# Norm chains of w_out moved under the following products, and first products of six weight pairs kept in DRAM, in a fused decoder layer

## Chip, cores and metric

The kernel runs on one core of a Trainium2 chip. The metric is the device time of one execution in microseconds.

## What is computed

One layer of a hybrid decoder for 1024 prompt tokens and 32 sample tokens (8 sequences of 4), 1056 columns in all, in float32. Two attention branches are merged to `m`, and then, cut to what the change touches:

```python
y = m @ w_out                                  # 1024 x 1024
x = x + gt_m * rmsnorm(y, g_post_mix)          # first norm
h2 = rmsnorm(x, g_pre_mlp) * (1 + sc_f) + sh_f # second norm
u = square(relu(h2 @ w_up))                    # 1024 x 4096
x = x + gt_f * rmsnorm(u @ w_down, g_post_mlp)
```

## The kernel before, in words

Everything here is kept with features on the 128 partitions and tokens along the columns. The 1056 tokens are two halves of TH = 528, each worked in two sub-chunks of TQ = 264 columns. A float32 product is three matmuls on operands split into a high and a low part (high by high, high by low, low by high). `raw_w` (L1224) loads weights on SP's queue into `raw`, of which there are three slots, and `split4` (L1229) makes the parts `ph` (a cast on ACT, L1233) and `pl` (a subtraction, L1235, two in three on POOL, the third on DVE), six slots each.

The stage has these parts, written in this order.

- For each half: the **w_out GEMM**. For each of 8 feature blocks and each sub-chunk, 24 matmuls (L1335 to L1337) go into one PSUM bank `ps_g`, of which there are three; such 24 are called a group. ACT copies a bank to Q (L1323) and squares it (L1325, L1328), POOL adds the squares to `ssq` (L1329).
- Then x of that half is loaded and turned by 40 transposes on PE into banks `ps_t` (L1348), copied on ACT (L1349).
- Then the **norm chain** of that half. `rstd` (L1255) sums `ssq` over partitions with PE products into `ps_o` (L1261), forms rv on DVE (L1262) and the power rt on POOL (L1263). `rstd_bc` broadcasts it with PE products into `ps_s` (L1275) and copies it to `r` on ACT (L1276). Then for 8 blocks: the scaling on DVE (`scaled`, L1286, and L1288 and L1282 for the sample columns), the add of x (L1355, in turn on DVE and POOL), the square on ACT (L1360) and its add to a second `ssq` (L1361, in turn POOL and DVE), and a store of x1 (L1363). Then the second sum and broadcast, 8 scalings, 8 shifts on ACT (L1368). `part` (L1305) splits an operand of 4 blocks by 528 columns into high (ACT, L1307) and low (DVE, L1308); the first half's two operands are split at the chain's end.
- The **up stage** works on 16 pairs of feature blocks of w_up by a Strassen-like scheme with 7 products per pair. A product (`product`, L1403) is 24 matmuls, 12 into each of two banks (L1410 to L1412). The first two products of a pair need only the first half's operands (0 and 1 in `hi`, `lo`), so `first_two` (L1419) forms them for the first PRE = 4 pairs ahead of the rest; it keeps the first in `s` in SBUF and reads the second with `s` added on DVE (L1431). `operands` (L1379) then builds the others (T1 to T4, B22) from both halves: one subtraction on POOL (L1383, t3), three on DVE (L1384 to L1386), each 2112 columns, then five `part`s. `pair` (L1436) does the other products: four sums S of the weights on DVE (L1439 to L1442), the products, reads (L1452 to L1458, L1483), relu and square on ACT (L1415, L1416) and a store to `d_u`. The weight pairs' banks come from all eight PSUM banks in turn (`bank8`).

Each engine takes its instructions in one order, set by a scheduler that goes by the written order, priorities and its own estimate of times; SP's queue holds all loads and stores here. A tile waits until its slot's last user is done, so a group of the GEMM waits until its bank was copied.

Of the kernel before, what the change touches and what calls it, by code (L numbers as in the profile page):

```python
# [18 lines left out]
P = 128  # L19
# [8 lines left out]
CQ = tuple((a, a + TQ) for a in range(0, T, TQ))  # L28
PRE = 4
NPC = 6  # L30
# [35 lines left out]
def hybrid_kernel(ctx: ExitStack, tc: tile.TileContext, ins, outs):  # L66
# [1224 lines left out]
    def mg_h(k, a, b):  # L1291
        return MG[a // TQ][0][:, k]
# [3 lines left out]

    TH = T // 2
    Q = []
# [10 lines left out]

    for th in range(2):  # L1310
        a, b = th * TH, (th + 1) * TH
        m = min(b, NP) - a
        Q.append([xs(qp, F32) for _ in range(2)])
        Y = lambda ft: Q[th][ft // 4][:, ft % 4]
        ssq = sums(npl, TH)
        for fp in range(4):
            wr = raw_w(w_out, 0, 8, fp * 2 * P, 2 * P)
            for ft in (2 * fp, 2 * fp + 1):
                pieces = [split4(wr[:, 4 * kh:4 * kh + 4, (ft % 2) * P:(ft % 2 + 1) * P]) for kh in range(2)]

                def evac(a_, b_, o):
                    c = slice(a_ - a, b_ - a)
                    act.copy(Y(ft)[:, c], o)  # L1323
                    if ft == 0:
                        act.activation(ssq[:, c], o, AF.Square)  # L1325
                    else:
                        sq = tl(npl, [P, TQ], F32, "sq", 2)
                        act.activation(sq, o, AF.Square)  # L1328
                        pool.tensor_tensor(ssq[:, c], ssq[:, c], sq, ALU.add)  # L1329

                for a_, b_ in CQ[2 * th:2 * th + 2]:
                    o = bank("g")[:, :TQ]
                    for k in range(8):
                        (wh, wl), kk = pieces[k // 4], k % 4
                        pe.matmul(o, wh[:, kk], mg_h(k, a_, b_), start=(k == 0), stop=False)  # L1335
                        pe.matmul(o, wh[:, kk], mg_l(k, a_, b_), start=False, stop=False)
                        pe.matmul(o, wl[:, kk], mg_h(k, a_, b_), start=False, stop=(k == 7))  # L1337
                    evac(a_, b_, o)
        xT = [xs(mgp if th else qp, F32) for _ in range(2)]
        for t0, t1 in tok_tiles(a, b):  # L1340
            w_ = t1 - t0
            for q in range(2):
# [6 lines left out]
                act.copy(xT[q][:, :, t0 - a:t1 - a], pt[:, :, :w_])  # L1349
        r = rstd_bc(npl, ssq, TH)  # L1350
        ssq2 = sums(npl, TH)
        for ft in range(8):
            y = Y(ft)
            scaled(y, r, gt_m, ft, m, TH)
            (pool if ft % 2 else dve).tensor_tensor(y, y, xT[ft // 4][:, ft % 4], ALU.add)  # L1355
            if ft == 0:
                act.activation(ssq2[:, :TH], y, AF.Square)
            else:
                sq = tl(npl, [P, TH], F32, "sq2", 2)
                act.activation(sq, y, AF.Square)  # L1360
                (dve if ft % 2 else pool).tensor_tensor(ssq2[:, :TH], ssq2[:, :TH], sq, ALU.add)  # L1361
            if ft % 4 == 3:
                sp.dma_start(d_x1[:, ft - 3:ft + 1, a:b], Q[th][ft // 4])  # L1363
        r2 = rstd_bc(npl, ssq2, TH)
        for ft in range(8):
            y = Y(ft)
# [7 lines left out]
    nps.close()  # L1374

    _mark(nc, "up")

# [14 lines left out]

    stg = ExitStack()
    sgp = stg.enter_context(tc.tile_pool(name="sgp", bufs=1, reuse_waits="tile"))
    bank_n = [0]

    def bank8():

        bank_n[0] += 1
        return bank("gggsstto"[bank_n[0] % 8])  # L1400

    SUB = ((0, TQ), (TQ, TH))

    def product(accs_, w, x, first):

        wh, wl = w
        for (s0, s1), acc in zip(SUB, accs_):
            o = acc[:, :TQ]
            for k in range(4):
                pe.matmul(o, wh[:, k], hi[x][:, k, s0:s1], start=first and k == 0, stop=False, skip_group_check=True)  # L1410
                pe.matmul(o, wh[:, k], lo[x][:, k, s0:s1], start=False, stop=False, skip_group_check=True)  # L1411
                pe.matmul(o, wl[:, k], hi[x][:, k, s0:s1], start=False, stop=k == 3, skip_group_check=True)  # L1412

# [4 lines left out]

    def first_two(i):  # L1419

        wr = raw_w(w_up, 0, 8, 2 * i * P, P)
        A11, A12 = split4(wr[:, 0:4]), split4(wr[:, 4:8])
        ab, bb = [bank8() for _ in SUB], [bank8() for _ in SUB]
        s = tl(sgp, [P, TH], F32, "s", PRE)
        c11 = tl(sgp, [P, TH], F32, "c", 3)
        product(ab, A11, 0, True)
        for (s0, s1), acc in zip(SUB, ab):
            act.copy(s[:, s0:s1], acc[:, :TQ])  # L1428
        product(bb, A12, 1, True)
# [3 lines left out]
        return s  # L1433

    def pair(i, s=None):
        wr = raw_w(w_up, 0, 8, 2 * i * P, 2 * P)  # L1436
# [22 lines left out]

        quad = lambda: tl(sgp, [P, TH], F32, "c", 3)  # L1460
        pre = s is not None
        if not pre:
# [28 lines left out]

    kept = [first_two(i) for i in range(PRE)]
    operands()
    for i in range(FF // (2 * P)):
        pair(i, kept[i] if i < PRE else None)
    stg.close()
    qps.close()
# [107 lines left out]
    def finish_cm(a, b, ssq):  # L1605
# [3 lines left out]
        x1 = load_x1(a, b)  # L1609
        r = rstd_bc(xw, ssq, n)  # L1610
        for ft in range(8):
# [54 lines left out]
```

## Time and profile before

| | us |
|---|---|
| median of 3 runs | 1942.78 |
| lowest, highest | 1940.33, 1943.16 |
| profiled execution | 1948.05 |
| its span | 1946.3 |
| PE busy | 1831.2 (94%) |
| DVE, ACT, POOL busy | 907.5 (47%), 860.6 (44%), 491.5 (25%) |

The span goes from the first profiled instruction to the last; the execution's own time holds 1.75 us more around it. A busy time is the union of an engine's instructions. An instruction's row gives its start counted from the span's start. The time of a matmul in a row holds its latency, so matmuls overlap: their pace is read from their starts or from a count in a window.

### The profile page before, as it was taken

Reading aid. Unit: us, or ns where it says so; the run is one execution under the profiler, and the core shown is the slowest. Engines: PE = TensorE matmul, PEld = TensorE weight load, DVE = VectorE, ACT = ScalarE, POOL = GpSimd, SP = SyncE. Lnnn points to the kernel's source line nnn. Section 1 sums busy time; section 2 is a strip of 40 time slices with the busy share of each in tenths; the row PEclk is TensorE's granted clock in tenths of the full one; section 3 lists DMA queues with packets and bytes.
Section 4 is the critical chain, followed back from the end, with each engine's and each line's share of the span. In section 5 each row is a group of like instructions: output and inputs, shape, how many; then the busy total and the mean of one; then the engine's idle time right before and its main releaser. Section 6 shows DMA issues by size and latency. Waiting matters only on the chain. (4 is left out here: it accounts for less than half of the span.)

```text
span 1946.3 us, 30982 instructions
## 1 busy us (share of the span) xinstructions
PE 1831.2 (94%) x12353; PEld 1723.1 (89%) x12353; DVE 907.5 (47%) x1907; ACT 860.6 (44%) x1553; POOL 491.5 (25%) x436
## 2 busy tenths in 40 slices
PE   6899999999999999999999494899999899999998
PEld 3888789998888999899999494899999799999997
DVE  3654545554455655544561416843333314344436
ACT  4556545657555434433124444555555531112212
POOL 3200010001233211101165344323222432222213
PEclk9899989999999999998999796999999899999999
DMA  8321422123547211353234322333233422222113
GB/s 268 77 68 59 149 77 77 54 75 111 175 165 217 78 49 57 106 177 120 58 101 162 132 77 87 102 100 121 95 100 121 172 88 89 88 101 98 67 42 138
DMA packets 178793, 209.09 MB, mean 107 GB/s; under 512 B 13908, under 2 KB 140432, under 8 KB 178648
## 3 DMA queue, kind: packets, MB, share of 16 engines
q1 hardware_dynamic: 173560, 190.13, 30.5%
q0 software_dynamic: 4864, 16.91, 2.6%
q8 instruction: 97, 1.59, 0.3%
q14 instruction: 48, 0.39, 0.1%
q10 hardware_dynamic: 224, 0.06, 0.0%
HBM read 163.40 MB, written 43.67 MB: 106 GB/s over the span
## 5 line engine op out<-in xcount | busy, mean ns | idle before, releaser
L404 PE MATMUL ps_g<-Xh,wh 128*128 128x352 f32 (+1 forms) x1176 | 393.7, 335 | 1.5 <-ACT wh L265 1.4
L406 PE MATMUL ps_g<-Xh,wl 128*128 128x352 f32 (+1 forms) x1176 | 390.4, 333 | 0.0
L405 PE MATMUL ps_g<-Xl,wh 128*128 128x352 f32 (+1 forms) x1080 | 356.7, 330 | 0.4 <-DVE Xl L347 0.4
L404 PEld LDWEIGHTS ps_g<-Xh,wh 128*128 128x128 f32 (+1 forms) x1176 | 222.7, 189 | 8.0 <-issue 3.0
L406 PEld LDWEIGHTS ps_g<-Xh,wl 128*128 128x128 f32 (+1 forms) x1176 | 221.8, 189 | 6.2 <-issue 4.2
L404 PE MATMUL ps_g<-uh,ph 128*128 128x352 f32 x672 | 218.0, 326 | 8.4 <-ACT uh L1518 7.7
L405 PE MATMUL ps_g<-ul,ph 128*128 128x352 f32 x672 | 216.8, 323 | 1.3 <-POOL ul L1519 1.3
L406 PE MATMUL ps_g<-uh,pl 128*128 128x352 f32 x672 | 216.5, 322 | 0.0
L405 PEld LDWEIGHTS ps_g<-Xl,wh 128*128 128x128 f32 (+1 forms) x1080 | 204.0, 189 | 5.9 <-issue 3.9
L1235 POOL TENSOR_TENSOR pl<-raw,ph 128x512 fp32r<-128x512 f32 x92 | 126.9, 1381 | 299.7 <-ACT ph L1233 299.7
L1233 ACT CAST ph<-raw 128x512 fp32r<-128x512 f32 x136 | 84.0, 621 | 253.1 <-PE ps_g L405 171.0
L266 POOL TENSOR_TENSOR wl<-wr,wh 128x1024 fp32r<-128x1024 f32 x26 | 63.1, 2425 | 441.8 <-ACT wh L265 295.2
L1534 DVE TENSOR_TENSOR acc<-acc,ps_g 128x352 f32<-128x352 f32 x144 | 74.0, 519 | 162.7 <-PE ps_g L406 150.6
L404 PEld LDWEIGHTS ps_g<-uh,ph 128*128 128x128 f32 x672 | 127.1, 190 | 9.6 <-ACT uh L1518 7.9
L405 PEld LDWEIGHTS ps_g<-ul,ph 128*128 128x128 f32 x672 | 127.2, 189 | 1.7 <-POOL ul L1519 1.7
L406 PEld LDWEIGHTS ps_g<-uh,pl 128*128 128x128 f32 x672 | 126.9, 189 | 0.0
L1410 PE MATMUL ps_g<-X,ph 128*128 128x264 f32 x340 | 98.4, 290 | 6.9 <-ACT s L1428 4.1
L1411 PE MATMUL ps_g<-X,ph 128*128 128x264 f32 x340 | 98.8, 291 | 2.3 <-DVE X L1308 2.3
L1412 PE MATMUL ps_g<-X,pl 128*128 128x264 f32 x340 | 98.3, 290 | 0.0
L1235 DVE TENSOR_TENSOR pl<-raw,ph 128x512 fp32r<-128x512 f32 x44 | 34.9, 793 | 126.5 <-ACT ph L1233 120.4
L1335 PE MATMUL ps_g<-X,ph 128*128 128x264 f32 x256 | 75.2, 294 | 17.0 <-ACT ssq L1325 10.8
L1235 POOL TENSOR_TENSOR pl<-S,ph 128x512 fp32r<-128x512 f32 x42 | 54.9, 1309 | 135.0 <-ACT ph L1233 135.0
(619 smaller groups left out, 4524.8 us busy)
## 6 DMA issues: line engine op xcount, KB each, us to landing
wr<-in_w_in SPq DMA_DIRECT2D x44, 512.0 KB
d_u<-c SPq DMA_DIRECT2D x64, 264.0 KB
ul<-d_u SPq DMA_DIRECT2D x32, 528.0 KB
wr<-in_w_ada SPq DMA_DIRECT2D x32, 512.0 KB
raw<-in_w_up SPq DMA_DIRECT2D x16, 1024.0 KB
raw<-in_w_down SPq DMA_DIRECT2D x16, 1024.0 KB
d_sg<-sgo SPq DMA_DIRECT2D x60, 176.0 KB
raw<-in_w_out SPq DMA_DIRECT2D x8, 1024.0 KB
```

Of the source, the lines that this page charges most:

```text
L266: (dve if lo_turn[0] % 2 else pool).tensor_sub(wl, wr, f(wh))
L404: pe.matmul(o, wh[:, k], rh(k, a, b), start=(k == 0), stop=False)
L405: pe.matmul(o, wh[:, k], rl(k, a, b), start=False, stop=False)
L406: last = pe.matmul(o, wl[:, k], rh(k, a, b), start=False, stop=(k == nk - 1))
L1233: act.copy(h_, src)
L1235: (dve if turn[0] % 3 == 0 else pool).tensor_sub(l_, src, f(h_))
L1335: pe.matmul(o, wh[:, kk], mg_h(k, a_, b_), start=(k == 0), stop=False)
L1410: pe.matmul(o, wh[:, k], hi[x][:, k, s0:s1], start=first and k == 0, stop=False, skip_group_check=True)
L1411: pe.matmul(o, wh[:, k], lo[x][:, k, s0:s1], start=False, stop=False, skip_group_check=True)
L1412: pe.matmul(o, wl[:, k], hi[x][:, k, s0:s1], start=False, stop=k == 3, skip_group_check=True)
L1534: dve.tensor_tensor(accs[a // 352](ft), accs[a // 352](ft), o, ALU.add)
```

## The change

- The norm chain of each half becomes a generator in steps (`norms`), and so do the transposes (`turn_x`). The steps of the first half's chain are written within the second half's GEMM, after the groups named in NORM_AT; those of the second half's within the first products, after the products named in NORM2_AT; the transposes after the second group of the blocks in XT_AT. `issue_after` holds a step's instructions behind the matmul given.
- The GEMM's banks are copied on DVE instead of ACT, and the squares read the copy.
- PRE goes from 4 to 6. `s` is stored to DRAM (`d_s`) and loaded again by `pair`. The first products use banks `g` and `t` alone.
- `raw` has two slots for three. One tag `n` of 8 slots of 528 columns and one tag `v` of 4 serve r, squares, s and c in both stages.
- `part` of the first half is called inside its chain, each operand as soon as its four blocks are done.

```diff
-PRE = 4
+PRE = 6
+NORM_AT = ((0, 0), (0, 1), (2, 1), (3, 1), (4, 0), (4, 1))
+XT_AT = (3, 4, 5, 6, 7)
+NORM2_AT = (0, 1, 4, 5, 6, 7)
...
-        wr = tl(w2p, [P, nk, n], F32, "raw", 3)
+        wr = tl(w2p, [P, nk, n], F32, "raw", 2)
...
+    def after(ins):
+        return tc.issue_after(ins) if ins is not None else nullcontext()
...
+    def norms(th):
+        rt = rstd(ssqs[th], TH)
+        yield
+        r = rstd_bc(npl, rt, TH)
+        ssq2 = sums(npl, TH)
         for ft in range(8):
-            y = Y(ft)
+            y = Y(th, ft)
             scaled(y, r, gt_m, ft, m, TH)
...
-                sq = tl(npl, [P, TH], F32, "sq2", 2)
+                sq = tl(npl, [P, TH], F32, "n", 8)
...
-        r2 = rstd_bc(npl, ssq2, TH)
+        yield
+        rt = rstd(ssq2, TH)
+        yield
+        r2 = rstd_bc(npl, rt, TH)
         for ft in range(8):
...
-        if th == 0:
-            for kq in range(2):
-                part(kq, Q[0][kq], qp, mgp)
+            if th == 0 and ft % 4 == 3:
+                part(ft // 4, Q[0][ft // 4], qp, mgp)
+        yield
...
-                    act.copy(Y(ft)[:, c], o)
+                    dve.tensor_copy(y, o)
...
-                        act.activation(sq, o, AF.Square)
+                        act.activation(sq, y, AF.Square)
...
+                    with after(last.ins):
+                        if (ft, si) in NORM_AT:
+                            next(chain, None)
+                        if si and ft in XT_AT:
...
+                            next(turns[th], None)
+        for _ in chain:
+            pass
+        for _ in turns[th]:
+            pass
+        chain = norms(th)
...
-    def first_two(i):
+    def first_two(i, n_):
...
-        ab, bb = [bank8() for _ in SUB], [bank8() for _ in SUB]
+        ab, bb = [bank8("gggtt") for _ in SUB], [bank8("gggtt") for _ in SUB]
...
+        last = product(ab, A11, 0, True)
+        step(last, 2 * n_)
...
+        last = product(bb, A12, 1, True)
+        step(last, 2 * n_ + 1)
...
+        sp.dma_start(d_s[n_], s)
...
+        if pre:
+            s = tl(npl, [P, TH], F32, "n", 8)
+            sp.dma_start(s, d_s[i])
...
+    def step(last, at):
+        if at in NORM2_AT:
+            with after(last):
+                next(chain, None)
...
-    kept = [first_two(i) for i in range(PRE)]
+    for i in range(PRE):
+        first_two(i, i)
+    for _ in chain:
+        pass
     operands()
```

The order of the instructions up to the middle of the first GEMM, and from the start of the down stage on, is the same in both. Between them it shows the move best at three places. In the rows that follow a tile carries its number, and the lines are those of the file they come from.

The first place is PE in the second GEMM, at the first chain's second sum (`ps_o`) and broadcast (`ps_s`). Before, they follow the transposes after the GEMM's third group:

```order
L1348 MATMUL ps_t_11637<-u_4_82,S_11635 128x128 x4
L1261 MATMUL ps_o_11045<-u_7_91,ssq_11003 128x1 x5
L1275 MATMUL ps_s_11056<-u_4_82,rt_11047 128x128 x4
L1275 MATMUL ps_s_11062<-u_4_82,rt_11047 128x16
L1335 MATMUL ps_g_11194<-X_9712,ph_11157 128x264
```

Now they stand at the end of the eleventh group (`ps_g_11468`), with one matmul between them:

```order
L1386 MATMUL ps_g_11468<-X_9710,ph_11464 128x264
L1387 MATMUL ps_g_11468<-X_9711,ph_11464 128x264
L1266 MATMUL ps_o_11248<-u_7_91,ssq_11072 128x1 x5
L1388 MATMUL ps_g_11468<-X_9710,pl_11465 128x264
L1279 MATMUL ps_s_11325<-u_4_82,rt_11250 128x128 x4
L1279 MATMUL ps_s_11331<-u_4_82,rt_11250 128x16
L1386 MATMUL ps_g_11497<-X_9712,ph_11460 128x264
```

So the sum moved behind eight more groups, and the broadcast has one matmul to cover rv and rt.

The second place is the queue that evacuates the GEMM's banks just after that broadcast. Before it is ACT, where the first copies of the second GEMM stand behind the shifts and the two casts:

```order
L1276 COPY r_11055<-ps_s_11062 128x16
L1368 ACTIVATE X_10365<-X_10365,mod_24_175 128x528 x4
L1368 ACTIVATE X_10366<-X_10366,mod_24_175 128x528
L1307 CAST X_11081<-X_10365 128x2112
L1368 ACTIVATE X_10366<-X_10366,mod_24_175 128x528 x3
L1307 CAST X_11085<-X_10366 128x2112
L1323 COPY X_11089<-ps_g_11103 128x264
```

Now it is DVE, where the copies of the ninth to eleventh group stand behind the eight scalings and the first low part:

```order
L1267 TENSOR_SCALAR rv_11249<-ps_o_11248 128x5
L1290 SCALAR_TENSOR_TENSOR X_10366<-X_10366,mod_25_176,n_11324 128x528 x4
L1290 SCALAR_TENSOR_TENSOR X_10367<-X_10367,mod_25_176,n_11324 128x528 x4
L1312 TENSOR_TENSOR X_11343<-X_10366,X_11342 128x2112
L1391 COPY X_10985<-ps_g_11386 128x264
L1391 COPY X_10985<-ps_g_11415 128x264
L1391 COPY X_10985<-ps_g_11468 128x264
L1312 TENSOR_TENSOR X_11355<-X_10367,X_11354 128x2112
```

So three copies passed from behind the whole chain on ACT to the middle of its last step on DVE.

The third place is DVE in the first products, at the first sum of squares of the second chain. Before, its adds are alone between the adds of x and rv:

```order
L1355 TENSOR_TENSOR X_11090<-X_11090,X_11626 128x528 x2
L1361 TENSOR_TENSOR ssq_11729<-ssq_11729,sq_2145_11740 128x528
L1361 TENSOR_TENSOR ssq_11729<-ssq_11729,sq_2147_11754 128x528
L1361 TENSOR_TENSOR ssq_11729<-ssq_11729,sq_2149_11769 128x528
L1361 TENSOR_TENSOR ssq_11729<-ssq_11729,sq_2151_11783 128x528
L1262 TENSOR_SCALAR rv_11788<-ps_o_11787 128x5
L1439 TENSOR_TENSOR S_12342<-raw_12340 128x512
```

Now the reads of the first pairs' second banks (`ps_t_11722` and on), a split and the S add of pair 0 stand among them:

```order
L1349 TENSOR_TENSOR X_10985<-X_10985,X_11359 128x528 x2
L1355 TENSOR_TENSOR ssq_11796<-ssq_11796,n_11807 128x528
L1467 TENSOR_TENSOR n_11725<-ps_t_11722,n_11724 128x264
L1467 TENSOR_TENSOR n_11725<-ps_t_11723,n_11724 128x264
L1355 TENSOR_TENSOR ssq_11796<-ssq_11796,n_11821 128x528
L1467 TENSOR_TENSOR n_11875<-ps_g_11872,n_11874 128x264
L1355 TENSOR_TENSOR ssq_11796<-ssq_11796,n_11836 128x528
L1467 TENSOR_TENSOR n_11875<-ps_t_11873,n_11874 128x264
L1239 TENSOR_TENSOR pl_12143<-raw_12136,ph_12142 128x512
L1355 TENSOR_TENSOR ssq_11796<-ssq_11796,n_11850 128x528
L1475 TENSOR_TENSOR S_12307<-raw_12305 128x512
L1267 TENSOR_SCALAR rv_11973<-ps_o_11972 128x5
```

So rv stands behind an add that needs pair 0's weights, and the banks of the second product are read after the chain's scalings and adds. On PE the fourth product's second bank (`ps_t_11873`) is the one of `ps_t_11722`.

## Rows read from the trace of the kernel before

**Rows 1.** The page's strip: the busy tenths of PE in forty equal slices of the span, 48.7 us each.

```profile
PE   6899999999999999999999494899999899999998
```

**Rows 2.** Windows, each with the busy time and the instructions of the engines, then PE's granted clock as a share of full speed, the share of the DMA engines and GB/s.

```profile
1087.84:1121.52 33.68, 6.78 (x37) 5.82 (x37) 20.58 (x23) 16.03 (x25) 11.99 (x9) 0.57 0.31 112
1121.52:1162.00 40.48, 40.48 (x315) 40.48 (x316) 4.54 (x5) 17.75 (x44) 21.31 (x22) 0.93 0.23 64
1175.22:1232.80 57.58, 26.58 (x160) 25.13 (x159) 40.70 (x79) 27.05 (x43) 25.86 (x14) 0.70 0.25 89
1260.00:1500.00 240.00, 240.00 (x1972) 240.00 (x1971) 84.43 (x159) 134.39 (x261) 70.71 (x55) 1.00 0.33 108
1500.00:1538.00 38.00, 37.87 (x311) 37.65 (x310) 8.13 (x17) 20.59 (x43) 11.62 (x10) 1.00 0.36 121
```

**Rows 3.** The waits of PE from 1024 to 1260 us: who waited for whom, us in total, times, the longest.

```profile
PE ps_o L1261 <- DVE ssq L1361: 33.2, 2, 19.8
PE ps_g L1335 <- ACT ssq L1325: 10.8, 1, 10.8
```

**Rows 4.** PE's timeline at the two chains: start, us from the first one's start to the last one's end, line, operation, tiles, count; in brackets the idle time before and what ended it. L1335 to L1337 are the w_out GEMM, L1348 the transposes of x, L1261 and L1275 the column sum and the broadcast, L1410 to L1412 the products of w_up.

```profile
1072.87 1.04 PE L1348 MATMUL ps_t<-u,S 128*128 128x128 f32 x8
1073.66 0.37 PE L1335 MATMUL ps_g<-X,ph 128*128 128x264 f32 x1
1073.87 0.50 PE L1261 MATMUL ps_o<-u,ssq 128*128 128x1 f32 x4
...
1108.07 2.61 PE L1275 MATMUL ps_s<-u,rt 128*128 128x128 f32 x10 [1.52 <-POOL rt L1263]
...
1121.91 0.42 PE L1336 MATMUL ps_g<-X,ph 128*128 128x264 f32 x1
1122.13 0.42 PE L1337 MATMUL ps_g<-X,pl 128*128 128x264 f32 x1
...
1169.88 1.38 PE L1275 MATMUL ps_s<-u,rt 128*128 128x128 f32 x10
...
1232.80 0.59 PE L1411 MATMUL ps_g<-X,ph 128*128 128x264 f32 x1 [2.32 <-DVE X L1308]
```

**Rows 5.** DVE's timeline in the first chain: L1286 the scalings, L1355 the adds of x, L1308 the low half of an operand.

```profile
1084.76 7.60 DVE L1286 SCALAR_TENSOR_TENSOR X<-X,mod,r 128x528 f32<-128x528 f32 x8
1092.28 4.76 DVE L1355 TENSOR_TENSOR X<-X,X 128x528 f32<-128x528 f32 x4
...
1110.93 5.52 DVE L1286 SCALAR_TENSOR_TENSOR X<-X,mod,r 128x528 f32<-128x528 f32 x8 [4.18 <-ACT r L1276]
1117.05 2.36 DVE L1308 TENSOR_TENSOR X<-X,X 128x2112 fp32r<-128x2112 f32 x1 [0.60 <-ACT X L1307]
```

**Rows 6.** ACT's timeline: the split of the second w_out load, then the copies of r and the first evacuation after the chain.

```profile
1027.14 1.14 ACT L1233 CAST ph<-raw 128x512 fp32r<-128x512 f32 x2 [0.78 <-DMA raw<-in_w_out]
...
1110.19 0.71 ACT L1276 COPY r<-ps_s 128x512 f32<-128x512 f32 x2 [7.49 <-PE ps_s L1275]
...
1120.80 0.37 ACT L1323 COPY X<-ps_g 128x264 f32<-128x264 f32 x1
```

**Rows 7.** POOL's timeline: a split, a partial sum of squares, four adds of x, and a split in the second chain.

```profile
1038.90 1.29 POOL L1235 TENSOR_TENSOR pl<-raw,ph 128x512 fp32r<-128x512 f32 x1 [2.03 <-ACT ph L1233]
1040.15 0.75 POOL L1329 TENSOR_TENSOR ssq<-ssq,sq 128x264 f32<-128x264 f32 x1
...
1088.51 6.72 POOL L1355 TENSOR_TENSOR X<-X,X 128x528 f32<-128x528 f32 x4 [6.34 <-ACT X L1349]
...
1175.84 1.26 POOL L1235 TENSOR_TENSOR pl<-raw,ph 128x512 fp32r<-128x512 f32 x1 [6.91 <-ACT ph L1233]
```

**Rows 8.** DVE's timeline in the second chain: L1286 and L1288 the scalings, L1361 the adds of the squares, L1431 the read of two banks into c, L1384 the first difference of the operands, L1439 to L1442 the S of a pair, L1308 the low half of T2.

```profile
1172.97 0.73 DVE L1286 SCALAR_TENSOR_TENSOR X<-X,mod,r 128x496 f32<-128x496 f32 x1
...
1175.86 1.28 DVE L1288 TENSOR_TENSOR X<-X,r 128x32 f32<-128x32 f32 x1
...
1186.78 0.69 DVE L1361 TENSOR_TENSOR ssq<-ssq,sq 128x528 f32<-128x528 f32 x1
...
1194.28 0.71 DVE L1361 TENSOR_TENSOR ssq<-ssq,sq 128x528 f32<-128x528 f32 x1 [1.47 <-POOL ssq L1361]
...
1203.02 0.73 DVE L1286 SCALAR_TENSOR_TENSOR X<-X,mod,r 128x496 f32<-128x496 f32 x1
...
1211.43 0.42 DVE L1431 TENSOR_TENSOR c<-ps_s,s 128x264 f32<-128x264 f32 x1
...
1217.51 3.43 DVE L1384 TENSOR_TENSOR X<-X,X 128x2112 f32<-128x2112 f32 x1 [4.23 <-POOL X L1383]
...
1221.21 1.44 DVE L1441 TENSOR_TENSOR S<-raw 128x512 f32<-128x512 f32 x1
...
1228.39 1.75 DVE L1442 TENSOR_TENSOR S<-raw,S 128x512 f32<-128x512 f32 x1
...
1230.40 2.34 DVE L1308 TENSOR_TENSOR X<-X,X 128x2112 fp32r<-128x2112 f32 x1
```

**Rows 9.** SP's queue: the first loads of w_out, and one period of the steady pairs.

```profile
1018.57 2.15 SPq L1226 DMA_DIRECT2D raw<-in_w_out  x3
...
1459.50 0.38 SPq L1226 DMA_DIRECT2D raw<-in_w_up  x1
1460.06 17.91 SPq L1417 DMA_DIRECT2D d_u<-c  x4
```

More of the change, by code (lines that the diff above doesn't have):

```diff
@@ L1308, in part, with turn_x @@
         dve.tensor_sub(lo[name], x, f(hi[name]))
-    for th in range(2):
-        a, b = th * TH, (th + 1) * TH
[L1312 to L1322, printed above, removed]
-                    act.copy(Y(ft)[:, c], o)
[L1324 to L1327, printed above, removed]
-                        act.activation(sq, o, AF.Square)
[L1329 to L1339, printed above, removed]
+    def after(ins):
+        return tc.issue_after(ins) if ins is not None else nullcontext()
+    Y = lambda th, ft: Q[th][ft // 4][:, ft % 4]
+    ssqs = {}
+    def turn_x(th):
+        a, b = th * TH, (th + 1) * TH
+        xT = xTs[th]
         for t0, t1 in tok_tiles(a, b):
@@ L1370, in hybrid_kernel @@
                 per_seq(y, y, sh_f, ft, m, TH, ALU.add)
-        if th == 0:
-            for kq in range(2):
-                part(kq, Q[0][kq], qp, mgp)
-    nps.close()
+            if th == 0 and ft % 4 == 3:
+                part(ft // 4, Q[0][ft // 4], qp, mgp)
+        yield
+    xTs, turns = {}, {}
+    chain = iter(())
+    for th in range(2):
+        a = th * TH
+        Q.append([xs(qp, F32) for _ in range(2)])
+        ssq = ssqs[th] = sums(npl, TH)
+        for fp in range(4):
+            wr = raw_w(w_out, 0, 8, fp * 2 * P, 2 * P)
+            for ft in (2 * fp, 2 * fp + 1):
+                pieces = [split4(wr[:, 4 * kh:4 * kh + 4, (ft % 2) * P:(ft % 2 + 1) * P]) for kh in range(2)]
+                for si, (a_, b_) in enumerate(CQ[2 * th:2 * th + 2]):
+                    o = bank("g")[:, :TQ]
+                    for k in range(8):
+                        (wh, wl), kk = pieces[k // 4], k % 4
+                        pe.matmul(o, wh[:, kk], mg_h(k, a_, b_), start=(k == 0), stop=False)
+                        pe.matmul(o, wh[:, kk], mg_l(k, a_, b_), start=False, stop=False)
+                        last = pe.matmul(o, wl[:, kk], mg_h(k, a_, b_), start=False, stop=(k == 7))
+                    c = slice(a_ - a, b_ - a)
+                    y = Y(th, ft)[:, c]
+                    dve.tensor_copy(y, o)
+                    if ft == 0:
+                        act.activation(ssq[:, c], y, AF.Square)
+                    else:
+                        sq = tl(npl, [P, TQ], F32, "v", 4)
+                        act.activation(sq, y, AF.Square)
+                        pool.tensor_tensor(ssq[:, c], ssq[:, c], sq, ALU.add)
+                    with after(last.ins):
+                        if (ft, si) in NORM_AT:
+                            next(chain, None)
+                        if si and ft in XT_AT:
+                            if th not in turns:
+                                xTs[th] = [xs(mgp if th else qp, F32) for _ in range(2)]
+                                turns[th] = turn_x(th)
+                            next(turns[th], None)
[4 more added lines that the diff above has]
+        chain = norms(th)
     _mark(nc, "up")
@@ L1391, in operands, with bank8 @@
         part("B22", B22, qp, qp)
-    stg = ExitStack()
-    sgp = stg.enter_context(tc.tile_pool(name="sgp", bufs=1, reuse_waits="tile"))
     bank_n = [0]
-    def bank8():
+    def bank8(which="gggsstto"):
         bank_n[0] += 1
-        return bank("gggsstto"[bank_n[0] % 8])
+        return bank(which[bank_n[0] % len(which)])
     SUB = ((0, TQ), (TQ, TH))
@@ L1432, in first_two, with pair @@
         u_out(c11, 2 * i, 0)
-        return s
-    def pair(i, s=None):
+        sp.dma_start(d_s[n_], s)
+    def pair(i, pre):
         wr = raw_w(w_up, 0, 8, 2 * i * P, 2 * P)
@@ L1458, in add @@
                 dve.tensor_tensor(c[:, s0:s1], acc[:, :TQ], tiles[what, n_], ALU.add)
-        quad = lambda: tl(sgp, [P, TH], F32, "c", 3)
-        pre = s is not None
+        quad = lambda: tl(npl, [P, TH], F32, "n", 8)
         if not pre:
@@ L1609, in finish_cm @@
         x1 = load_x1(a, b)
-        r = rstd_bc(xw, ssq, n)
+        r = rstd_bc(xw, rstd(ssq, n), n)
         for ft in range(8):
```

29 lines of the change are left out of this document (15 added, 14 removed).

## The prediction

> **What bounds the kernel now.** I read the page's strip of forty slices first: PE is the bound, busy for nine tenths or more of nearly every slice, and outside the ramps at both ends its two worst slices, the 23rd and the 25th with a 4, lie in the stage that the change touches [rows 1]. Cutting that stage into windows says what is lost there [rows 2]. From 1260 to 1500 us, in the steady pairs, PE is never idle: 1972 matmuls of 264 columns in 240 us, 0.122 us each, so a group of 24 into one PSUM bank is 2.92 us. From 1087.84 to 1121.52 PE works 6.78 us of 33.68, and from 1175.22 to 1232.80 26.58 of 57.58. The two losses are the two norm chains, one for each half of the tokens. The waits name what PE sat for: 33.2 us for the sum of squares, 10.8 for an ACT evacuation that stood behind the chain [rows 3].
>
> PE's timeline fixes two anchors [rows 4]. The first w_out GEMM ends by about 1073.0. At 1232.80 PE starts the first matmul that had waited for the low half of T2. Between them lie 159.8 us: 89.0 to 1162, where the second GEMM ends, and 70.8 after it. In the same rows matmuls follow each other by 0.22 us after a long wait, against 0.12 otherwise; the granted clock was 0.57 in the first idle window and 0.70 in the second [rows 2], that is, partly at the lower level of 1.2 GHz.
>
> **The change, first piece (first chain, under the second GEMM).** PE's work is the same; only where it stands moves.
> - The first GEMM now carries its 40 transposes. Eight take 0.79 us, from 1072.87 to 1073.66 [rows 4], so 40 take 4.0.
> - The second GEMM is 16 groups, 46.7 us, with another 40 transposes, 4.0, and two rounds of column sum and broadcast. At full clock 4 of the 10 sum products take 0.50 with their latency, so some 0.9 for 10 in a stream, and the 10 of the broadcast 1.3 [rows 4]: a round is 2.2 and two 4.4. Together 55.1.
> - The first scaling of the chain stands on DVE ahead of the evacuation of the second GEMM's fourth group, with the first add: 8 scalings of 0.95 and an add of 1.19, as they ran beside POOL adds [rows 5], and the new PSUM copy. For that copy the bounds are 0.37, ACT's copy of the same tile [rows 6], and 0.42, DVE's read of the same bank shape [rows 8]; I take 0.42, the same engine. From the broadcast's end DVE needs 0.8 + 7.6 + 1.2 + 0.4 = 10.0, and PE has 19 matmuls and two groups in the other banks, 8.1. Wait: 1.9.
> - The sum of squares alternates DVE and POOL, 2.18 us for each pair of adds (0.71 on DVE after a wait of 1.47 for POOL, [rows 8]). r comes 12.5 us into the second GEMM (three groups, five matmuls, one round, the copy); scalings and adds take 12.4, copies and a split between them 3, the seven adds 7.2: 35.1. PE's sum products stand behind 11 groups, 8 transposes, a round and the 1.9, at 37. So the 13.4 and 19.8 us waits for it have no successor here. The broadcast follows after one matmul, so the 1.5 us for rv and rt stays [rows 4].
> - Then the old wait comes back on another engine. The next group needs a bank whose copy is now on DVE, behind the eight scalings and the first `L1308` subtraction. Before, ACT held it. From the broadcast's end at 1110.68 that subtraction ended at 1119.41 [rows 5]; with the copy the wait is 9.2, for 10.84 before. Right after that wait PE did 315 matmuls in 40.48 us [rows 2], 2.1 more than at 0.122; I keep 2.1.
> Sum: 4.0 + 55.1 + 1.9 + 1.5 + 9.2 + 2.1 = 73.8, for 89.0. **Gain 15.2.**
>
> **Second piece (second chain, under the first products).** Twelve products of 24 matmuls (2.92 each) replace eight. Four of them, 96 matmuls, were done later: 11.7 us of work that disappears behind the second anchor. The length itself goes by the chain, not by PE:
> - 67 matmuls, sum and broadcast until r: 8.2 + 2.2, then the copy of r, 0.7 [rows 6]: 11.1.
> - From the first scaling to the last add of the sum the chain took 22.0 (1172.97 to 1194.99, [rows 8]). It stays: 33.2. Under it PE runs 17 matmuls past the broadcast and then stands, since the second product's banks are read on DVE behind scalings and adds: 14.5 (to 1187.47) + 0.4 later. That idle time of about 14 us lies beside the chain and costs only what it makes PE late at the sum: 12 matmuls at 0.22 and 39 at 0.122 bring it there at 33.5; the sum is done at 34.4.
> - DVE now has an S add of pair 0 ahead of rv. Its weights are loaded into a slot freed by the last split of the fifth pair's first products, which stands just behind the read of the fourth product's second bank: at about 30. The first use of the second 1 MB load came 8.6 us after issue of the first (1018.57 to 1027.14, [rows 6, 9]); with two 1 MB stores of x1 ahead I take 8.6: 38.6. S add 0.7, as an add of that width [rows 8], rv and rt 1.5 [rows 4]: 40.8. Broadcast and r [rows 4, 6]: 2.0. So 42.8.
> - From the first scaling to T2's low half: 29.7 (1203.02 to 1232.74, [rows 8]), of which DVE waits 4.23 for POOL's t3 and spends 3.43 on the first operation on 2112 columns and 2.34 on the last. DVE has about as much between: six reads of banks, five S adds, one split. So 72.5, for 70.8. **Loss 1.7.** PE runs out of first products at about 57 and idles 15.
>
> **At no cost.** ACT gives up 32 copies of 0.37 and is not the bound. Six stores and six loads of 264 KB for s: bounds 0 and 8.6 us each (the two 1 MB loads above); s is stored at least two products before it is read, and one pre-formed pair is 14.6 us of PE, so 0. Two more 512 KB loads of w_up go under the same cover. `raw` with two slots for three: the last w_up load is issued at 1459.50 [rows 9], its pair starts 20.4 (168 matmuls) before PE's end of that stage at 1538, so the lead is 58 us. One slot less makes it 38, against 8.6. The change of stage to down keeps its wait, since its rows stand as before.
>
> **Sum: 15.2 - 1.7 + 11.7 = 25.2.** The profiled execution took 1948.05 (span 1946.3, the rest around it); it becomes 1922.9. The median of the runs is 5.3 below the profiled time, so the forecast is 1942.8 - 25.2 = **1917.6**. Bounds: without the 1.9, with the S add on time (the broadcast then follows its 34 matmuls, 2.2 earlier), and with the last part 6 shorter (two S adds of 1.44 and 1.75 back at 0.69, and the wait of 4.23 for POOL hidden, [rows 8]), the gain is 35; with contention at its worst (rival 1) and another 4 for weights, 8.
>
> **Rule against row.** At 1175.86 a DVE operation on 32 columns took 1.28 us, where one on 496 columns takes 0.73, while POOL's split ran from 1175.84 for 1.26 [rows 7, 8]; eight scalings took 7.60 beside POOL and 5.52 without [rows 5]. The Trainium skill, "SBUF — State Buffer", Who interferes with whom, says that a DVE instruction with two SBUF inputs and a GpSimd instruction that reads SBUF exclude each other for the whole instruction, whichever began first; these rows agree. By that rule the sum would be the first rival's 1930.6.
>
> **The rivals.**
> 1. *The two engines shut each other out.* The first chain now shares its time with five splits (1.29), four adds (1.68) and five partial sums (0.75) on POOL [rows 7]: 17 us, of which 4 are in my rows already. If all the rest delays the chain, its sum comes 13 us later and PE waits for it: 1917.6 + 13 = 1930.6. For it: the rows just named. Against it: both queues have gaps in which they can pass each other, and PE's place for the sum leaves 2 us.
> 2. *The last part shrinks.* If the operands follow the scaling with little between, 29.7 falls towards 22, and 1917.6 becomes 1907 to 1911. Against it: DVE's list is about as long as before.
> 3. *Slower: weights late on two slots.* The S adds and splits are in DVE's and ACT's line, so a late load stops everything behind it, in every pair. The gain is gone when 14 pairs each wait 1.8 us, and 4 us each gives 1917.6 + 56 = 1974. It decides when a load lands over 38 us after its slot comes free, plus what SP's stores hold it up; SP does issue it behind a train of d_u stores that spans 18 us [rows 9]. 18 + 8.6 is still below 38.
> 4. *The chains move and nothing is won*, because every bank wait grows as the chain shrinks: within 3.9 us of before. Against it: 96 matmuls of cover and 33 us of waits for the sum are real.
>
> **How the numbers follow.** My forecast, 1910 to 1926: 0.58. Rival 1, 1926 to 1936: 0.20. Rival 2: 0.10. Rival 4: 0.05. Rival 3: 0.07. About 0.2%, 3.9 us, is what a measurement of this kernel can tell from no change. Faster 0.88, same 0.05, slower 0.07. The range takes in the forecast and most of rivals 1 and 2: 1904 to 1934.
>
> **What would show it.** Right: PE still has a wait of some 9 us in the second GEMM, now released by a DVE copy; one near 14 in the first products, released by a DVE read; one near 15 before T2; none over 3 for the first chain's sum. Wrong: a long wait for the first chain's sum (rival 1); ACT or DVE idle on DMA into raw between 1260 and 1500, and PE idle there (rival 3); a second piece well under 70 us (rival 2).

## The result, and the profile after

The changed kernel takes 1929.99 us in the median of 16 runs, the kernel before 1945.53 in 16; the ratio is 0.9912, with a 95% interval of 0.9889 to 0.9935. By that ratio it is 17 us less (13 to 22), for 25 forecast. One of the 16 runs of the changed kernel took 6233.76 us at a granted clock of 0.365; the ratio leaves it out, and why that run was slow is not shown. The profiled execution of the changed kernel took 1938.06 us (span 1936.4).

Before any stage is read: the code ahead of the first w_out GEMM is the same in both kernels and in every experiment below, and it takes 1011.5 to 1038.8 us in their profiles (last section). So a difference of a few us cannot be read from a span. Instead I cut each profile at four instructions and compare lengths: **first piece**, from the first matmul of the first w_out GEMM to the end of the last of the second; **second piece**, from there to the end of the first low-half subtraction on DVE in `operands` (T2's); **rest of up**, to the last product; **down**, to the end. The changed kernel profiled twice (the second time as control, below) agrees with itself to 1.2 us in each piece.

| us | before | change | control |
|---|---|---|---|
| ahead (same code) | 1024.9 | 1029.9 | 1026.5 |
| first piece | 137.1 | 128.5 | 127.3 |
| second piece | 70.8 | 75.5 | 75.8 |
| rest of up | 305.1 | 294.2 | 294.0 |
| down | 408.5 | 408.2 | 407.9 |
| sum without "ahead" | 921.5 | 906.5 | 904.9 |

The strip of the page, as [rows 1]. The 23rd and 25th slice had a 4; the lowest in this stage are now a 6 and two 7:

```profile
PE   6899999999999999999998976799999899999998
```

PE's waits from 1010 to 1260 us, as [rows 3] (who waited for whom, us in total, times, the longest):

```profile
PE ps_g L1386 <- DVE X L1391: 13.3, 2, 9.3
PE ps_t L1443 <- DVE n L1467: 13.2, 1, 13.2
PE ps_g L1443 <- ACT X L1311: 12.1, 1, 12.1
PE ps_g L1386 <- ACT ph L1237: 5.9, 1, 5.9
PE ps_s L1279 <- POOL rt L1268: 4.1, 2, 2.8
```

The 33.2 us for the sum of squares have left the list. What came in their place is what the forecast named: a copy of a GEMM bank on DVE (13.3, in two waits), the read of a first product's bank on DVE (13.2), and the operands ahead of T2 (12.1). The 5.9 is the wait for the first w_out weights, as before; it lies ahead of the first piece.

Windows of the changed kernel, columns as in [rows 2]: the first GEMM, the second, the second piece, then the stretches behind the two waits for a bank copy.

```profile
1029.85:1082.30 52.45, 52.45 (x417) 52.20 (x418) 12.14 (x22) 21.77 (x44) 28.50 (x27) 0.96 0.48 158
1082.30:1158.35 76.05, 61.45 (x465) 60.53 (x466) 40.90 (x49) 35.33 (x65) 42.38 (x36) 0.87 0.30 95
1158.35:1233.94 75.59, 46.40 (x343) 44.72 (x342) 52.65 (x97) 34.77 (x63) 34.81 (x21) 0.81 0.40 131
...
1107.07:1115.82 8.75, 8.75 (x50) 8.75 (x51) 7.33 (x9) 6.39 (x14) 6.82 (x7) 0.66 0.74 247
1138.61:1144.70 6.09, 6.09 (x31) 6.09 (x32) 4.51 (x5) 4.19 (x9) 4.41 (x3) 0.58 0.00 0
```

In the last two rows PE is busy throughout and yet does 50 matmuls in 8.75 us and 31 in 6.09. At the 0.122 of [rows 2] they would take 6.1 and 3.8: each of these two waits costs 2.3 to 2.7 us more than its own length, at a granted clock of 0.66 and 0.58, that is, mostly at the lower level of 1.2 GHz.

DVE in the changed kernel, as [rows 5] and [rows 8]: first the scalings of the first chain and the copy that stands behind them, then the second round of scalings with the three copies behind it, then the second chain from the S add of pair 0.

```profile
1095.18 10.78 DVE L1290 SCALAR_TENSOR_TENSOR X<-X,mod,n 128x528 f32<-128x528 f32 x8 [1.75 <-ACT n L1280]
1105.88 0.70 DVE L1349 TENSOR_TENSOR X<-X,X 128x528 f32<-128x528 f32 x1
1106.50 0.42 DVE L1391 COPY X<-ps_g 128x264 f32<-128x264 f32 x1
...
1129.73 5.52 DVE L1290 SCALAR_TENSOR_TENSOR X<-X,mod,n 128x528 f32<-128x528 f32 x8 [3.21 <-ACT n L1280]
1135.86 2.36 DVE L1312 TENSOR_TENSOR X<-X,X 128x2112 fp32r<-128x2112 f32 x1 [0.60 <-ACT X L1311]
1138.13 1.10 DVE L1391 COPY X<-ps_g 128x264 f32<-128x264 f32 x3
...
1198.53 0.69 DVE L1475 TENSOR_TENSOR S<-raw 128x512 f32<-128x512 f32 x1 [6.01 <-issue]
1199.14 0.16 DVE L1267 TENSOR_SCALAR rv<-ps_o 128x5 f32<-128x5 f32 x1
...
1203.43 6.28 DVE L1290 SCALAR_TENSOR_TENSOR X<-X,mod,n 128x496 f32<-128x496 f32 x8
...
1221.41 3.40 DVE L1419 TENSOR_TENSOR X<-X,X 128x2112 f32<-128x2112 f32 x1 [2.18 <-POOL X L1418]
1224.74 1.74 DVE L1478 TENSOR_TENSOR S<-raw,S 128x512 f32<-128x512 f32 x1
```

Eight scalings of the same shape take 10.78 us in one place and 5.52 in the other. In the second POOL does nothing; in the first it works through splits and adds of x with one gap, of 0.64 us:

```profile
1096.47 1.31 POOL L1239 TENSOR_TENSOR pl<-raw,ph 128x512 fp32r<-128x512 f32 x1 [1.71 <-ACT ph L1237]
1097.74 1.79 POOL L1349 TENSOR_TENSOR X<-X,X 128x528 f32<-128x528 f32 x1
1099.49 1.75 POOL L1239 TENSOR_TENSOR pl<-raw,ph 128x512 fp32r<-128x512 f32 x1
1101.20 1.79 POOL L1349 TENSOR_TENSOR X<-X,X 128x528 f32<-128x528 f32 x1
1103.64 1.75 POOL L1349 TENSOR_TENSOR X<-X,X 128x528 f32<-128x528 f32 x1 [0.64 <-DVE X L1290]
```

### The profile page after: what moved, and what is told of

It is laid out like the page before. It is cut to its first block, busy times and chain, and to the rows that moved or that the text cites. A ratio compares the mean times of both kernels' runs of the same rounds, so it can differ in the third digit from the quotient of the medians.

```text
span 1936.4 us, 31063 instructions
## 1 busy us (share of the span) xinstructions
PE 1835.9 (95%) x12353; PEld 1727.2 (89%) x12353; DVE 933.3 (48%) x1951; ACT 847.0 (44%) x1509; POOL 498.4 (26%) x436
## 4 chain that ended last, share of the span: by engine, by line
PE 87%; DVE 4%; DMA 4%; issue 1%; ACT 1%; POOL 1%; SPq 1%; DVEq 0%; POOLq 0%; ACTq 0%
PE ps_g L408 17%; PE ps_g L410 17%; PE ps_g L409 17%; PE ps_g L1444 2%; PE ps_g L1443 2%; PE ps_g L1445 2%; PE ps_s L684 2%; PE ps_t L709 2%; PE ps_g L1386 2%; PE ps_g L1387 2%; PE ps_g L1388 2%; PE ps_t L1444 1%; PE ps_t L1445 1%; PE ps_t L1443 1%; PE ps_s L681 1%
## 5 line engine op out<-in xcount | busy, mean ns | idle before, releaser
L270 POOL TENSOR_TENSOR wl<-wr,wh 128x1024 fp32r<-128x1024 f32 x26 | 63.2, 2429 | 442.7 <-ACT wh L269 293.9
L1443 PE MATMUL ps_g<-X,ph 128*128 128x264 f32 x376 | 108.4, 289 | 12.1 <-ACT X L1311 12.1
L1444 PE MATMUL ps_g<-X,ph 128*128 128x264 f32 x376 | 108.8, 290 | 0.5 <-DVE X L1312 0.5
L1445 PE MATMUL ps_g<-X,pl 128*128 128x264 f32 x376 | 108.2, 288 | 0.0
L1386 PE MATMUL ps_g<-X,ph 128*128 128x264 f32 x256 | 77.4, 302 | 19.2 <-DVE X L1391 13.3
L269 ACT CAST wh<-wr 128x1024 fp32r<-128x1024 f32 x52 | 54.5, 1047 | 75.7 <-PE ps_g L409 55.0
```

Source lines behind the costliest of these rows:

```text
L269: act.copy(wh, wr)
L270: (dve if lo_turn[0] % 2 else pool).tensor_sub(wl, wr, f(wh))
L1445: last = pe.matmul(o, wl[:, k], hi[x][:, k, s0:s1], start=False, stop=k == 3, skip_group_check=True)
```

## The experiments

Experiment 1 changes nothing, 2 to 9 change one thing each in the changed kernel (5 with several edits), 10 and 11 combine; kernel 3 is the kernel of experiment 3, and so on. The scheduler orders each kernel anew, so other instructions can change place too. The table gives the lengths by the cuts above, and the interval of the ratio to the kernel before, run beside it on the same chip (1 to 4, 5 to 8 and 9 to 11 on three chips). For noise: in the kernels whose edits lie behind the first piece it is 127.2 to 128.9 (1, 3, 4, 7, 9 and the change), and the two profiles of the changed kernel differ by 0.3 in the second.

| | first | second | rest of up | sum | median | ratio |
|---|---|---|---|---|---|---|
| control (1) | 127.3 | 75.8 | 294.0 | 904.9 | 1927.74 | 0.9848 to 0.9935 |
| first chain at its old place (2) | 142.1 | 78.5 | 293.9 | 922.6 | 1945.59 | 0.9985 to 1.0048 |
| 4 pairs (3) | 128.5 | 68.3 | 306.0 | 910.5 | 1934.16 | 0.9917 to 0.9983 |
| 8 pairs (4) | 128.6 | 77.2 | 284.0 | 898.5 | 1918.84 | 0.9832 to 0.9912 |
| finer steps (5) | 114.5 | 77.2 | 294.4 | 895.0 | 1923.45 | 0.9854 to 0.9944 |
| adds of x on DVE (6) | 128.7 | 75.8 | 294.0 | 906.6 | 1934.77 | 0.9906 to 0.9965 |
| S adds late (7) | 128.9 | 74.9 | 293.1 | 905.0 | 1931.69 | 0.9903 to 0.9969 |
| copies on ACT (8) | 130.2 | 75.5 | 294.4 | 907.6 | 1924.24 | 0.9823 to 0.9974 |
| t3 on DVE (9) | 127.2 | 73.7 | 293.4 | 903.3 | 1926.16 | 0.9893 to 0.9949 |
| 5 + 9 with 8 pairs (10) | 114.1 | 75.4 | 285.9 | 884.3 | 1901.55 | 0.9752 to 0.9829 |
| 5 + 9 with 10 pairs (11) | 114.9 | 73.9 | 284.0 | 882.2 | 1900.85 | 0.9752 to 0.9822 |

**1. The changed kernel again.**

> The changed kernel again, as a control. Its profile so far had 128.5 us from the first matmul of the first w_out GEMM to the last of the second (137.1 before), and 75.6 us from there to the first matmul on the low half of T2 (70.8 before). Theory A (the gain is made of these stage lengths): both lengths within 2 us again, the time within 1920 to 1940 by the granted clock of the stages that no edit touches. Theory B (the missing 8 us of the forecast are a chance of that one profiled execution): one of the two lengths is 5 us or more shorter this time.

Both lengths came back within 1.2 us: theory A. The missing 8 us are no accident of one execution.

**2. The first chain between the two GEMMs.**

```diff
         chain = norms(th)
+        if th == 0:
+            for _ in chain:
+                pass
```

> The first chain back between the two GEMMs, everything else as in the changed kernel. Theory A: the first piece alone is worth 8.5 us by the two profiles, so the length from the first GEMM's start to the second's end goes from 128.5 back to 136 to 138 and the time to 1938 or so. Theory B (the predicted 15.2 were there and were lost elsewhere, in the clock of later stages): 1945. If the chain's place is worth nothing: 1930.

PE's wait for the sum of squares is back:

```profile
PE ps_o L1266 <- DVE ssq L1355: 19.9, 1, 19.9
```

The first piece is 142.1, longer than before the change. Three groups of the second GEMM stand ahead of the chain's second sum, as before, but the transposes now lie inside the two GEMMs: the first takes 52.4 us for 48.2, and from the end of the last wait the second takes 42.9 for 40.4. The sum rises by 17.7 against the control, the median by 17.9, twice what theory A said. So in this kernel the first chain's place is worth 17.7 us, and without it nothing is left of the gain (921.5 before, 922.6). It is not the whole gain over the kernel before, though: of the control's 16.6 us, 9.8 lie in the first piece and 6.1 in the second piece with the rest of up (369.8 for 375.9); here these two are 372.4, the second piece being 2.7 longer than the control's with another order on DVE.

**3 and 4. Four pairs, eight pairs.**

```diff
-PRE = 6
+PRE = 4
```

and `PRE = 8` in the other.

> First products of four pairs ahead instead of six. Theory A (the second piece's length is that of the chain, 96 matmuls lie in PE's idle time): 75.6 us stay, PE's idle time before T2 grows from 12 to about 24, the time grows by 11.7 to 1941.7. Theory B (the eight reads of banks and the casts of these products on DVE and ACT lengthen the chain): the piece shrinks by 3 to 5, the time is 1937 to 1939.

> First products of eight pairs ahead. Theory A: four more products lie in PE's idle 12 us before T2, so 11.7 less; and the S add of pair 0 no longer stands ahead of rv on DVE, so the second piece is 2 to 4 shorter: 1914 to 1918. Theory B (DVE's list of reads sets T2): the second piece grows by 4 or more and the time is 1922 or more.

The four products give back 12.0 behind T2 (306.0 to 294.0), but the second piece is 7.5 shorter without them: worth 4.5 us by these two lengths, 5.6 by the sums, and my 11.7 needed a piece that does not care. It shrinks by more than theory B's 3 to 5, and the median, 1934.16, is below both theories' times. With four pairs, as before the change, the second piece and the rest of up come to 374.3 for 375.9: moving the second chain, with all that goes with it, brings some 1.6 us without more pairs. In kernel 3 DVE starts the last scalings 44.0 us into the piece and ends T2's low half 24.3 later; in the changed kernel it is 45.1 and 30.5. DVE in kernel 3:

```profile
1195.96 6.27 DVE L1290 SCALAR_TENSOR_TENSOR X<-X,mod,n 128x496 f32<-128x496 f32 x8
...
1210.80 2.36 DVE L1419 TENSOR_TENSOR X<-X,X 128x2112 f32<-128x2112 f32 x1 [4.83 <-POOL X L1418]
```

The engines' window of that piece, 68.32 us, columns as in [rows 2]:

```profile
1151.96:1220.28 68.32, 34.15 (x246) 32.82 (x246) 48.00 (x92) 28.94 (x51) 28.95 (x18) 0.74 0.33 114
```

PE is idle for half of it and DVE for 20 us, so no engine is full over the whole piece. What differs is DVE's list in its last part: with six pairs, four more S adds, four more reads of banks and a split stand between the scalings and T2, and some of these and the first operation on 2112 columns run longer beside POOL's splits (3.40 us for 2.36). With eight, 10.0 more leave the rest of up, and the piece grows by only 1.4; in this kernel's order no S add stands ahead of rv. In sum 6.4 less; the median, 1918.84, lies between the two theories' values.

**5. Finer steps of the first chain.**

```diff
-NORM_AT = ((0, 0), (0, 1), (2, 1), (3, 1), (4, 0), (4, 1))
+NORM_AT = ((0, 0), (0, 1), (1, 0), (1, 1), (2, 0), (3, 1), (4, 0), (4, 1), (5, 0), (5, 1))
...
+            if th == 0 and ft in (1, 3, 5):
+                yield
...
-                    dve.tensor_copy(y, o)
+                    cp = dve.tensor_copy(y, o)
...
-                    with after(last.ins):
+                    with after(last.ins), after(cp.ins):
```

The `yield` stands at the end of the body of both loops of scalings.

> The first chain's two rounds of scalings cut into steps of two blocks, one after each group, each step's DVE work held behind that group's copy; place of the steps a little earlier. Theory A (the 4.0 and 9.3 us of PE's waits in the second GEMM are bank copies that stand behind eight scalings, and the slow matmuls after each wait, 5 to 6 us, come with them): both waits fall under 2 us, the length from the first GEMM's start to the second's end goes from 128.5 to 110 to 115, the time to 1912 to 1917. Theory B (the chain's own length sets it, since DVE's work is the same): the waits move to the sum of squares or to the first products, and the time stays within 4 us of 1930.

PE's waits in the first piece, beside the 6.0 for the first weights:

```profile
PE ps_g L1390 <- DVE X L1395: 3.7, 1, 3.7
PE ps_s L1279 <- POOL rt L1268: 2.9, 1, 2.9
PE ps_o L1266 <- DVE ssq L1355: 0.2, 1, 0.2
```

(The 2.9 and the 0.2 lie in the second piece.) One bank wait of 3.7 is left of 13.3, the first chain's rv and rt are covered, and the piece is 114.5, theory A's number: 10.9 us of PE's idle time went, and 2 to 3 us more with them, as much as one slow stretch. The second piece grew by 1.4 to 1.7. At its start, 1135.87, now lies the first chain's last low half on DVE:

```profile
1136.26 2.35 DVE L1312 TENSOR_TENSOR X<-X,X 128x2112 fp32r<-128x2112 f32 x1
```

In the changed kernel both low halves are done 16 us ahead of the piece. The second chain's first scaling follows 14.0 us into the piece, for 11.6 in the changed kernel; that the shifted work is the reason is likely, but no run isolates it. By the cuts the kernel is 10 us faster than the control; the two medians alone, 1923.45 and 1927.74, would not separate them.

**6. Adds of x on DVE.**

```diff
-            (pool if ft % 2 else dve).tensor_tensor(y, y, xT[ft // 4][:, ft % 4], ALU.add)
+            (pool if th and ft % 2 else dve).tensor_tensor(y, y, xT[ft // 4][:, ft % 4], ALU.add)
```

> In the first chain all eight adds of x on DVE, none on POOL. Theory A (DVE and POOL shut each other out: the eight scalings took 10.78 us beside five POOL instructions, 5.52 alone): the scalings take 6 to 8.5, PE's wait of 4.0 us for the bank copy falls to about 2 and the slow stretch after it goes or shortens, so the length to the second GEMM's end falls by 2 to 5. Theory B (no exclusion, the scalings are slow for another reason): the scalings stay at 10 to 11, the extra adds, 2.8 us, lie ahead of the copies and the wait grows to 5 or more.

The scalings, and what they ran beside on POOL now:

```profile
1104.10 7.61 DVE L1290 SCALAR_TENSOR_TENSOR X<-X,mod,n 128x528 f32<-128x528 f32 x8 [1.75 <-ACT n L1280]
```

```profile
1105.39 3.03 POOL L1239 TENSOR_TENSOR pl<-raw,ph 128x512 fp32r<-128x512 f32 x2 [1.71 <-ACT ph L1237]
```

10.78 became 7.61, and the first bank wait 1.45 for 4.00. Against the 5.52 with POOL idle, both come to 1.05 us more for each POOL instruction beside them (five, and now two). So POOL beside it is what makes the scalings slow; theory A holds for them. It does not pay, though: the sum of squares now comes late (a wait of 3.1 us for `ssq`, which the changed kernel does not have), and the first piece stays at 128.7, not the 2 to 5 shorter that theory A said.

**7. S adds of pairs 0 and 1 behind the second chain's last scaling.**

```diff
-        dve.tensor_tensor(S[0], a21, a22, ALU.add)
...
+        with after(at):
+            dve.tensor_tensor(S[0], a21, a22, ALU.add)
...
```

All four sums of S are in the block, and `at` is the chain's last DVE instruction for these two pairs.

> The S adds of pairs 0 and 1 held on DVE behind the last scaling of the second chain. Theory A (the S add that waits for weights sits ahead of rv and delays r by some 6 us): PE's broadcast comes 4 to 6 us earlier, the first scaling of the last step too, and the second piece falls from 75.6 to 70 to 73. Theory B (DVE's total work up to T2 sets the piece): r comes earlier but T2 within 1.5 us of before, since the same S adds are now between the scalings and T2.

Theory B: the piece is 0.9 shorter. The last scalings start 41.3 us into the piece for 45.1, and the S adds that used to stand ahead of them now stand behind, one of them beside POOL's t3. DVE, then POOL:

```profile
1193.27 4.92 DVE L1479 TENSOR_TENSOR S<-S,raw 128x512 f32<-128x512 f32 x1
1198.11 0.68 DVE L1480 TENSOR_TENSOR S<-raw 128x512 f32<-128x512 f32 x1
```

```profile
1192.57 5.06 POOL L1420 TENSOR_TENSOR X<-X,X 128x2112 f32<-128x2112 f32 x1 [11.34 <-DVE X L1288]
```

A subtraction of 0.68 us that began 0.7 after t3 takes 4.92 and ends 0.6 after it: it waits out the whole of the other instruction and then does its own work. The Trainium skill, "SBUF — State Buffer", section Who interferes with whom, says that a DVE instruction with two SBUF inputs contends with a GpSimd instruction that reads SBUF, and that the contention is an exclusive lock; this pair is the plainest case of it in these traces.

**8. Bank copies on ACT.**

```diff
-                    dve.tensor_copy(y, o)
+                    act.copy(y, o)
```

> The GEMM's banks copied on ACT, as before the change; the squares still read the copy. Theory A (the 4.0 us wait is DVE's, ahead of which stand eight scalings): that wait goes, ACT's order has only the copies of r and two casts there; the wait of 9.3 becomes one for ACT behind eight shifts and two casts, 9 to 11. Net 4 to 6 less, 1924 to 1926. Theory B (ACT fills up with copies, squares and casts and the chain's squares come late): PE waits for the sum of squares and the time is 1932 or more.

The first wait shrinks to 1.7, the second is 10.5 on ACT, and a wait of 3.4 for the sum of squares appears: 130.2, no gain. ACT's list holds the chain's squares, shifts and casts as DVE's holds its scalings, so the copy waits on either.

**9. t3 on DVE.**

```diff
-        pool.tensor_tensor(t3, B22, B12, ALU.subtract)
+        dve.tensor_tensor(t3, B22, B12, ALU.subtract)
```

> t3, the first difference of the operands, on DVE instead of POOL. Theory A (POOL's 4.98 us on 2112 columns shuts DVE out while it runs and slows what begins beside it): t3 takes 2.4 on DVE, the operations behind it 2.36 and 0.68 instead of 3.40 and 1.74, T2's low half comes 3 to 5 us earlier, the second piece goes from 75.6 to 71 to 73. Theory B (DVE's list alone sets T2): 2.4 more in it, the piece is 75.6 to 78.

```profile
1207.26 2.34 DVE L1418 TENSOR_TENSOR X<-X,X 128x2112 f32<-128x2112 f32 x1
...
1210.76 1.74 DVE L1478 TENSOR_TENSOR S<-raw,S 128x512 f32<-128x512 f32 x1 [0.48 <-POOL pl L1239]
1212.42 2.35 DVE L1419 TENSOR_TENSOR X<-X,X 128x2112 f32<-128x2112 f32 x1
```

t3 takes 2.34 on DVE, less than POOL's 4.98, and the first operation behind it 2.35 for 3.40; the S add between them stays at 1.74. The piece is 73.7: 2 us shorter, in direction theory A, short of its size.

**10 and 11. The edits together.** Finer steps and t3 on DVE, with `PRE = 8` and `PRE = 10`.

> Three edits together: the finer steps of the first chain, t3 on DVE, first products of eight pairs. Theory A (they act in different places and add): from the first GEMM's start 906 us become 906 - 13 (finer) - 8 (eight pairs) - 3 (t3) = 882, the median some 24 below the changed kernel, 1904 to 1908. Theory B (the shorter first piece and the earlier T2 only let PE wait elsewhere): 1912 or more.

> As the one with eight pairs, with ten. Theory A (PE still has some 15 us idle in the second piece, to be filled by four more products, 11.7): another 6 to 9 less, 1896 to 1900. Theory B (T2 waits for DVE, whose list gets two more pairs' reads and splits, and PE has no idle time left): within 3 us of the one with eight.

They add, theory A of the first text: 884.3 with eight pairs and 882.2 with ten, for the control's 904.9. Ten pairs are 2 us better than eight by the cuts, and the medians do not tell them apart: theory B of the second text. Either is some 42 us below the kernel before (ratio 0.979), and by the cuts 21 to 23 below the control. PE's waits that are left with ten pairs:

```profile
PE ps_t L1447 <- DVE n L1471: 14.3, 1, 14.3
PE ps_g L1390 <- ACT ph L1237: 6.1, 1, 6.1
PE ps_g L1447 <- DVE n L1471: 4.0, 1, 4.0
PE ps_g L1390 <- DVE X L1395: 3.7, 1, 3.7
```

## Why the prediction was right, and where its sizes were off

Forecast 1917.6, measured 1929.99: inside the stated range of 1904 to 1934, faster as said, by two thirds of the 25.2. It is outside the 1910 to 1926 that I gave 0.58, and inside what I gave rival 1. Of the 12.4 us, 2.7 are the starting point: I took 1942.78 for the kernel before, from 3 runs, and 16 give 1945.53. The mechanism was right and the sizes were not. Term by term, with the profile of the change:

- **First piece, 15.2 forecast, 8.6 measured (9.8 in the control).** The waits came where they were put: 1.30 us for rv and rt (1.5 forecast), 9.29 for the bank behind eight scalings and a low half (9.2), none for the sum. Two sizes failed. The first bank wait is 4.00 for 1.9, because the scalings take 10.78, not the 7.6 of [rows 5]: that row had POOL beside part of them, here POOL ran beside all of them. Experiment 6 shows the cause of the slow scalings. And I charged slow matmuls, 2.1, behind one wait; there are two such stretches, 2.7 + 2.3 by their windows. These make 5 of the missing 6.6; in the other 1.6 PE is busy, 1.3 of it in the second GEMM, and I have no row for it.
- **Second piece, loss of 1.7 forecast, 4.7 measured.** Step by step: the wait on the first bank read is 13.2 (14 forecast), PE comes to the sum 34.4 us into the piece (33.5), the S add that stands ahead of rv runs at 40.2 (38.6), the last scalings start at 45.1 (42.8), and from there to T2's low half it is 30.5 (29.7). Every step is there; the lateness grows from 0.9 to 2.3 us, and the last stretch adds 0.8. The S add is as near as this by some luck: its load was issued at 1191.93, 33.6 us into the piece, for the 30 at which I had its slot free, and was used 6.6 later, for 8.6.
- **Four products in front, 11.7 forecast, 10.9 measured** (305.1 to 294.2). The term is right as written, but my sentence that the length of the second piece "goes by the chain, not by PE" hid its price. T2's low half is done 24 us after the last scalings start with four pairs and 30 with six; with the later start the piece is 7.5 longer (experiment 3), so 7 of the 11.7 are paid back in it, most of that on DVE's list. With rows of before, where that stretch was 29.7 with four pairs, I could not see that it was about to shrink and be filled again; rival 2 described the shrinking.
- **At no cost.** In the steady pairs PE is never idle: from 1233.89 to 1528.11 it is busy for 294.17 of 294.22 us:

```profile
1233.89:1528.11 294.22, 294.17 (x2394) 293.96 (x2394) 118.13 (x211) 157.92 (x295) 85.35 (x66) 0.99 0.35 112
```

The two raw slots and the stores and loads of s cost nothing that shows; there is nothing for rival 3.

**Rival 1**, at 1930.6, has the measured time and half of the mechanism, so its number is luck. DVE and POOL do shut each other out (experiments 6 and 7), but the sum of squares did not come late and PE never waited for it. The lock is paid at a bank copy, in the first step of the chain, 2 us and a slow stretch; the 3.0 us lost in the second piece are the small steps above. Rival 4 is out: the ratio's interval ends at 0.9935.

Not settled: no run has the second chain alone back at its old place, so the 1.6 us of its move rest on lengths from experiment 3 and the kernel before.

## What to carry to other kernels

Moving a serial chain beside a GEMM pays where the GEMM waited for it, but the engine that runs the chain must not also hold the GEMM's bank copies behind a whole step: cut the steps so that each copy passes between them, which gave another 13 to 14 us in the first piece here, 10 in sum. Price elementwise work by rows in which the other engine is as busy as it will be. And count what moved-up work puts into the list of the engine that ends the stretch: here four products that filled PE's idle time gave 12.0 us behind T2 and cost 7.5 ahead of it, most of that on DVE.

## What the runs showed of the hardware

The same instructions ahead of the stage take 1011.5 us in one profile and 1038.8 in another. Two of these profiles, 25 us apart, kernel 7's window first, then kernel 6's, columns as in [rows 2]:

```profile
0.00:1013.46 1013.46, 974.72 (x6289) 877.26 (x6289) 533.92 (x1301) 494.31 (x885) 185.68 (x209) 0.99 0.36 112
```

```profile
0.00:1038.83 1038.83, 999.37 (x6290) 895.76 (x6290) 535.54 (x1301) 494.55 (x885) 186.18 (x209) 0.96 0.36 110
```

Counts agree, DVE, ACT and POOL are busy for the same time within 2 us, and only PE's busy time differs, by 25 us, with the granted clock at 0.99 and 0.96. From 800 to 1000 us, nearly the same stretch of the program, where PE is busy for 197 of 200 us in both, it is 0.97 in one and 0.88 in the other, with 1361 matmuls and 1219:

```profile
800.00:1000.00 200.00, 197.00 (x1361) 183.37 (x1360) 104.47 (x276) 63.14 (x118) 49.54 (x42) 0.97 0.42 128
```

```profile
800.00:1000.00 200.00, 197.58 (x1219) 181.16 (x1218) 96.87 (x255) 63.55 (x110) 34.14 (x26) 0.88 0.38 117
```

PE's idle time differs by less than 1 us (38.7 and 39.5). So a lower granted clock goes with the longer time and no longer wait; what lowered it is not shown. The single runs agree: the changed kernel's shortest took 1920.42 us at a mean clock of 0.973, and one of 1940.67 had 0.961. That is why single times of one kernel lie 20 us apart, and why stage lengths between two instructions, which repeat to 1 to 2 us, tell more than medians here.
